# One matrix product per mamba group: three products of split parts in place of one in full fp32

## The chip, the cores and the metric

The kernel runs on one core of a Trainium2 chip. A core has a matrix engine (TensorE, PE in the profile), a vector engine (VectorE, DVE), a scalar engine (ScalarE, ACT), GpSimd (POOL) and a queue for transfers (SyncE, SP). Each takes its own instructions strictly in the order in which they stand in its queue; semaphores make one engine wait for another or for a transfer. The metric is device time in microseconds: 1594.79 us before (median of 3 runs, 1594.73 to 1595.04).

## The reference

A two-layer encoder on 256 tokens of width 2048: layer 1 is a mamba block, layer 2 a forgetting attention. The part that matters is the mamba block, in chunks of 64 tokens in the reference and of two tiles of 128 tokens in the kernel:

```python
proj = h @ w_in                       # z, x, B, C and dt
xbc = silu(conv(x, B, C))
...
cb = einsum('bclgn,bcsgn->bclsg', cm, bm)
y_diag = einsum('bclsgr,bcsgrp->bclgrp', cb[..., None] * lmat, xdt)
...
y_off = einsum('bclgn,bcgrpn->bclgrp', cm, prev) * exp(acs)[..., None]
...
y = gated_group_rmsnorm(y, z, norm_w)
return y @ w_out
```

There are 8 groups of 8 heads. All is fp32 and has to agree with the reference to fp32 accuracy.

## The kernel before

The work is a list of parts that `run` walks through. A part is a bundle of products on PE, of some 1.4 to 2.8 us, and weights are prepared three halves ahead: a transfer brings `raw` (or sums of weights, `sum_a`, `sum_b`, `sum_c`, which POOL's queue builds by adding transfers), ACT rounds it to the format fp32r into `wh`, DVE takes the rest, `wl = raw - wh`, and PE multiplies `wh` and `wl`. An fp32r product takes one pass on PE; three of them, high times high, high times low and low times high, stand for one product in fp32. `act_hi` and `dve_lo` are these two steps.

The side work of a mamba group, which lies between these products, is put off by `later(n, fn)`: it is issued n double steps of parts later. What stands in which order on an engine is then set by a scheduler, which walks through the program with its own estimate of times and puts an instruction where its inputs and its buffers are free; so a tile's buffer, too, sets an instruction's place. Buffers of a tag go round (`bufs`), and a writer waits until all who read the buffer's last tile are done.

A group g goes like this:

- B, C and four blocks of x are projected (`pst`), joined and convolved (`rest`, `cu`, `BT`, `CT`, `xT`); `rest` has 2 buffers.
- `load_acs(i)`, i = 0 to 3, lets POOL's queue load `acsB`: sums of decays of two heads, spread over the 128 partitions, 128x512 fp32, from a buffer in memory. The tag `acsB` has 2 buffers.
- `decay(i)`: ACT makes `ee` out of `acsB` with four activations (Relu, 128x128 each) and one Exp (128x512). The tag `ee` has 3 buffers. DVE multiplies it with `cb`.
- `y_pe(i)`: PE multiplies `ee` and `xd` in fp32 (`py`).
- `off_pe`: the product this document is about. For the second tile of 128 tokens, the part of the output that comes from the first tile: `pof = cb[:, 128:256].T @ xg`, 128x128 by 128x512, in fp32. `xg` is x times step and decay; the middle part of `cb` is C of the second tile times B of the first.
- `off_dve`: `pof` times a decay (`yo`) is added to `xa`.
- z is projected (`psa`), ACT takes its tanh (`zth`, two instructions), DVE makes `zs` of it; `gate(t)` adds `py` to `xa`, multiplies by `zs`, and ACT sums its squares (`junkg`, one for each tile of tokens); `norm` makes the factor `gv` on DVE and POOL; ACT scales `xa` twice; `out_pe` transposes `xa` on PE (`pyt`).

Parts of the next group's projections, and from the third group on of the output projection (`sum_units`, tiles `psx`, `psz`, `psv`), run on PE around all this. The mamba layer takes about the first 650 us.

Of the kernel before, what the change touches and what calls it, by code (L numbers as in the profile page):

```python
# [12 lines left out]
F32R = mybir.dt.float32r  # L13
# [4 lines left out]
P = 128  # L18
# [49 lines left out]
def hybrid_kernel(ctx: ExitStack, tc: tile.TileContext, a):  # L68
    nc = tc.nc

    def pool(name, bufs, **kw):
        return ctx.enter_context(tc.tile_pool(name=name, bufs=bufs, **kw))
# [6 lines left out]
    sp = pool("side", 2)  # L79
# [5 lines left out]
    lp = phase.enter_context(tc.tile_pool(name="mamba", bufs=1))  # L85
# [13 lines left out]
    def bank(p, name):  # L99
        return p.tile([P, 512], F32, tag=p.name, name=name)  # L100

    def act_hi(out, in_, scale=None):
        if scale is None:
            nc.scalar.activation(out, in_, AF.Copy)  # L104
        else:
            nc.scalar.activation(out, in_, AF.Copy, scale=scale)

    def dve_lo(out, in_, hi, scale=None):
        if scale is None:
            return nc.vector.tensor_tensor(out, in_, hi.bitcast(F32), op=ALU.subtract)  # L110
        return nc.vector.scalar_tensor_tensor(
            out, in_, scale, hi.bitcast(F32), op0=ALU.mult, op1=ALU.subtract)
# [10 lines left out]
    def later(n, fn):  # L123

        events.setdefault(now[0] + 2 * n, []).append(fn)
# [114 lines left out]
    def unit_both(src, n, x, post):  # L240


        u = {"src": src, "w": [None], "both": (2 * n, n)}

        def mm(h):
            if h == 0:
                u["ps"] = bank(psm, "pst")
            for k in range(8 * h, 8 * h + 8):
                product(u["ps"][:2 * n], u["w"][0][0][:, 2 * n * k:2 * n * k + 2 * n],
                        ktile(x(), k).rearrange("p i s -> p (i s)"), start=k == 0,  # L250
                        stop=k == KT - 1)

        parts = [{"u": u, "h": [0], "mm": lambda h=h: mm(h)} for h in range(2)]
        parts[1]["post"] = lambda: post(u["ps"])
        return parts
# [129 lines left out]
    def per_token(ps, n, scale, bias, done):  # L385


        vt = sp.tile([P, S], F32, tag="cu", name="vt")
        joined(vt[:2 * n, :], ps, scale)

        def rest():
            pt = bank(psa, "pvt")
            for t in range(T2):
                nc.tensor.matmul(pt[:, t * n:(t + 1) * n], vt[:2 * n, t * P:t * P + P],
                                 cst[:2 * n, C_S[n]:C_S[n] + n], start=True, stop=True)
            v = small.tile([P, T2, 64], F32, tag="v", name="v", bufs=1)[:, :, :n]
            nc.vector.tensor_tensor(
                v, pt[:, :T2 * n].rearrange("p (t h) -> p t h", t=T2),
                bias.unsqueeze(1).to_broadcast([P, T2, n]), op=ALU.add)
            done(v)  # L400
        later(2, rest)
# [151 lines left out]
    def group_units(g):  # L553
        st = {"acs": {}}
# [31 lines left out]
        def post_x(i):  # L586
            def post(ps):
                conv_silu(ps, 6 * g + 2 + i, f"xT{g}_{i}", lambda o: x_done(i, o))
                later(2 + wait, lambda: load_acs(i))
            return post  # L590
# [7 lines left out]
        def x_done(i, o):  # L598
            st[f"x{i}"] = o
            if g == 0:  # L600
                later(1 + wait, lambda: xa_pe(i))
                later(2 + wait, lambda: xa_dve(i))
            elif i % 2:
                st["first"], st["then"] = ((cb_pe,), (cb_dve, lambda: st["mul0"]())) if i == 1 else (
                    (lambda: y_pe(0), lambda: y_pe(1)), ())
                later(2, lambda: [f() for f in (lambda: xa_pe(i - 1), lambda: xa_pe(i),
                                                *st["first"])])
                later(3, lambda: [f() for f in (*st["then"], lambda: xa_dve(i - 1),
                                                lambda: xa_dve(i))])
            later(2 + wait + more, lambda: decay(i))  # L610
            if g == 0:
                later(4 + wait + more, lambda: y_pe(i))
            if i == 3:
                if g > 0:
                    later(5, lambda: [y_pe(2), y_pe(3)])
                late = wait + more or 1
                later(4 + late, off_pe)
                later(5 + late, off_dve)

        def xa_pe(i):  # L620
            st[f"pxa{i}"] = pt = bank(psa, "pxa")
            for t in range(T2):
                nc.tensor.transpose(pt[:, t * P:t * P + P], st[f"x{i}"][:, t * P:t * P + P],
                                    ident)

        def xa_dve(i):
            if i == 0:
                xa = lp.tile([P, 4 * (S + 1)], F32, tag="xa", name=f"xa{g}", bufs=2)
                st["xa"] = xa[:, :T2 * 512].rearrange("p (t c) -> p t c", t=T2)
                xd = lp.tile([P, 4 * (S + 1)], F32, tag="xd", name=f"xd{g}")  # L630
                st["xd"] = xd[:, :T2 * 512].rearrange("p (t c) -> p t c", t=T2)
                st["xg"] = lp.tile([P, 512], F32, tag="xg", name=f"xg{g}")
            c = slice(i * P, i * P + P)
            pt = st[f"pxa{i}"]
            pt4 = pt[:, :S].rearrange("p (t h d) -> p t h d", t=T2, h=2)
            d = dts[:, :, H0 + 2 * i:H0 + 2 * i + 2].unsqueeze(3).to_broadcast([P, T2, 2, HD])
            nc.vector.tensor_tensor(
                st["xd"][:, :, c].rearrange("p t (h d) -> p t h d", h=2), pt4, d, op=ALU.mult)
            nc.vector.tensor_tensor(
                st["xg"][:, c].rearrange("p (h d) -> p h d", h=2), pt4[:, 0],  # L640
                heads_of(gdt, i, 1), op=ALU.mult)
            nc.vector.tensor_tensor(
                st["xa"][:, :, c].rearrange("p t (h d) -> p t h d", h=2), pt4,
                heads_of(row[:, R_D:R_D + MH], i, T2), op=ALU.mult)

        def decay(i):
            ee = lp.tile([P, 2, T2, P], F32, tag="ee", name="ee", bufs=3)
            for j in range(2):
                h = H0 + 2 * i + j
                for t in range(T2):  # L650
                    nc.scalar.activation(ee[:, j, t, :], st["acs"][i][:, j, t * P:t * P + P],
                                         AF.Relu, scale=-1.0, bias=beta[:, t, h:h + 1])
            nc.scalar.activation(ee, ee, AF.Exp, scale=-1.0)

            def mul():
                cb = st["cb"].rearrange("p (b l) -> p b l", b=3)
                nc.vector.tensor_tensor(
                    ee, ee, cb[:, 0:3:2, :].unsqueeze(1).to_broadcast([P, 2, T2, P]), op=ALU.mult)
                st[f"m{i}"] = ee
            if g > 0 and i == 0:  # L660
                st["mul0"] = mul
            else:
                later(1, mul)

        def y_pe(i):
            if i == 0:
                st["py"] = [bank(psa, f"py{t}") for t in range(T2)]
            m = st[f"m{i}"]
            for j in range(2):
                hl = 2 * i + j  # L670
                c = slice(hl * HD, hl * HD + HD)
                for t in range(T2):
                    nc.tensor.matmul(st["py"][t][:, c], m[:, j, t, :], st["xd"][:, t, c],  # L673
                                     start=True, stop=True)

        def off_pe():
            st["pof"] = bank(psa, "pof")
            nc.tensor.matmul(st["pof"], st["cb"][:, P:2 * P], st["xg"], start=True, stop=True)  # L678

        def off_dve():  # L680
            yo = sp.tile([P, 512], F32, tag="zth", name="yo")
# [585 lines left out]


    groups = [group_units(g) for g in range(G)]
    parts = groups[0] + groups[1]  # L1270
    for g in range(0, SUMMED, 2):
# [5 lines left out]
    def out_f(g):  # L1277
# [3 lines left out]
    f = unit_both(a["wf_f"], FH, lambda: lay2["x"], lambda ps: later(1, lambda: per_token(  # L1281
        ps, FH, lay2["rstB"], row[:, R_F:R_F + FH], forget)))
# [98 lines left out]
```

## Time and profile before

| | us |
|---|---|
| runs, median (lowest to highest) | 1594.79 (1594.73 to 1595.04) |
| the profiled execution | 1594.61 |
| its span, first to last instruction | 1592.8 |
| PE busy | 1578.4 |
| DVE busy | 1333.6 |
| ACT busy | 1062.1 |
| POOL busy | 164.3 |

The profiled execution took 1.8 us more than its span and 0.18 us less than the median. The page gives busy times, the chain of work that ended last, and groups of instructions; views of the trace give the waits, the timeline of each engine, the chain piece by piece, and busy time by stretches. Times inside the trace are counted from the start of the span. A matrix product in fp32 shows as two instructions on PE, one in fp32r as one. L678 is line 678 of the kernel before.

### The profile page before, as it was taken

The numbers are of one execution on the slowest core, as the hardware profiler recorded it, in microseconds if no ns is written. First come the engines' busy times: TensorE is split into PE (matmuls) and PEld (weight loads), VectorE is DVE, ScalarE is ACT, GpSimd is POOL, SyncE is SP. The second block draws the span as 40 slices with busy tenths as digits, with TensorE's granted clock in tenths as the row PEclk, the third lists the DMA queues.
The fourth block names the chain that finished last, engine by engine and source line by source line (L and its number), as shares of the span: only waits on it lengthen the run. The fifth ranks groups of instructions, "written<-read, shape, count | busy, mean of one in ns | idle before, by whom it ended". The sixth has DMA issues, their size and how long they took to land.

```text
span 1592.8 us, 22603 instructions
## 1 busy us (share of the span) xinstructions
PE 1578.4 (99%) x7807; PEld 1328.2 (83%) x7807; DVE 1333.6 (84%) x2016; ACT 1062.1 (67%) x1624; POOL 164.3 (10%) x211
## 2 busy tenths in 40 slices
PE   8999999999999999999999999999999999999997
PEld 6888888888888888878888888888888888888886
DVE  6998989798979898798887887878878887888886
ACT  7677776767676765766776675666666666667663
POOL 0000111011100110011110110110110111011100
PEclk9999999999999999999999999999999999999999
DMA  9665798769986987579887887797886887888842
GB/s 360 214 215 185 185 275 220 260 177 275 221 265 174 274 220 237 188 168 260 262 236 254 220 214 250 224 247 215 221 258 189 249 256 180 237 263 239 266 156 80
DMA packets 100355, 361.76 MB, mean 227 GB/s; under 512 B 11504, under 2 KB 12144, under 8 KB 100112
## 3 DMA queue, kind: packets, MB, share of 16 engines
q1 hardware_dynamic: 75312, 270.82, 48.4%
q0 software_dynamic: 24784, 89.24, 29.3%
q8 instruction: 61, 1.00, 0.2%
q14 instruction: 54, 0.44, 0.1%
q10 hardware_dynamic: 144, 0.26, 0.1%
HBM read 358.08 MB, written 2.20 MB: 226 GB/s over the span
## 4 chain that ended last, share of the span: by engine, by line
PE 97%; DMA 2%; DVE 0%; issue 0%; ACT 0%; POOL 0%; SPq 0%; ACTq 0%; POOLq 0%
PE psa L130 24%; PE pst L130 16%; PE psx L130 12%; PE psz L130 10%; PE psv L130 9%; PE psu L130 8%; PE psy L130 8%; PE py L673 2%; PE pqk L1108 1%; PE psc L1126 1%; PE ppt L1162 1%; DMA cst<-in_consts 1%; DMA xs<-in_x 1%; PE pof L678 0%; PE po L1188 0%; PE psc L1124 0%
## 5 line engine op out<-in xcount | busy, mean ns | idle before, releaser
L104 ACT ACTIVATE wh<-raw 128x1024 fp32r<-128x1024 f32 (+1 forms) x371 | 391.8, 1058 | 209.9 <-PE psa L130 63.9
L110 DVE TENSOR_TENSOR wl<-raw,wh 128x1024 fp32r<-128x1024 f32 (+2 forms) x371 | 447.6, 1213 | 61.3 <-issue 30.0
L104 ACT ACTIVATE wh<-sum_a 128x1024 fp32r<-128x1024 f32 x176 | 185.8, 1057 | 134.1 <-PE psy L130 28.4
L110 DVE TENSOR_TENSOR wl<-sum_a,wh 128x1024 fp32r<-128x1024 f32 x176 | 214.9, 1223 | 61.8 <-PE psu L130 41.4
L130 PE MATMUL pst<-x,wh 128*128 128x512 f32 (+1 forms) x800 | 205.3, 397 | 3.0 <-ACT wh L104 1.8
L130 PEld LDWEIGHTS pst<-x,wh 128*128 128x128 f32 (+1 forms) x800 | 146.0, 189 | 33.7 <-ACT wh L104 2.5
L130 PE MATMUL psa<-wh,x 128*128 128x512 f32 x512 | 129.3, 392 | 0.0
L104 ACT ACTIVATE wh<-sum_b 128x1024 fp32r<-128x1024 f32 x88 | 93.3, 1060 | 51.9 <-PE psx L130 29.9
L110 DVE TENSOR_TENSOR wl<-sum_b,wh 128x1024 fp32r<-128x1024 f32 x88 | 106.6, 1221 | 10.4 <-issue 9.4
L130 PEld LDWEIGHTS pst<-x,wl 128*128 128x128 f32 x768 | 106.4, 191 | 9.8 <-DVE wl L110 1.6
L130 PEld LDWEIGHTS psa<-wh,x 128*128 128x128 f32 x512 | 95.4, 188 | 20.3 <-issue 0.5
L130 PE MATMUL pst<-x,wl 128*128 128x256 f32 x768 | 109.6, 284 | 0.4 <-DVE wl L110 0.4
L177 POOL DMA_DIRECT2D sum_a<-in_wf_s x64 | 56.0, 876 | 469.9 <-DVE wl L110 293.3
L130 PE MATMUL psz<-wh,x 128*128 128x512 f32 x256 | 100.4, 392 | 0.0
L130 PE MATMUL psv<-wh,x 128*128 128x512 f32 x256 | 99.8, 390 | 0.0
L130 PE MATMUL psu<-wh,x 128*128 128x512 f32 x256 | 99.7, 390 | 0.0
L130 PE MATMUL psy<-wh,x 128*128 128x512 f32 x256 | 99.7, 389 | 0.0
L766 DVE TENSOR_TENSOR xs<-psa,xs 128x512 f32<-128x512 f32 (+1 forms) x81 | 52.0, 680 | 31.7 <-PE psa L130 31.6
L130 PE MATMUL psa<-wh,ghf 128*128 128x512 f32 (+1 forms) x260 | 71.0, 392 | 0.0
L130 PE MATMUL psa<-wh,glf 128*128 128x512 f32 (+1 forms) x260 | 69.6, 386 | 0.0
L130 PE MATMUL psa<-wl,ghf 128*128 128x512 f32 (+1 forms) x260 | 69.6, 386 | 0.0
L130 PE MATMUL psa<-wl,x 128*128 128x512 f32 x256 | 69.0, 390 | 0.0
(360 smaller groups left out, 3251.8 us busy)
## 6 DMA issues: line engine op xcount, KB each, us to landing
raw<-in_wf_p SPq DMA_DIRECT2D x128, 512.0 KB, 4.8
raw<-in_wm_t SPq DMA_DIRECT2D x90, 512.0 KB, 4.9
raw<-in_wm_z SPq DMA_DIRECT2D x64, 512.0 KB, 5.7
sum_a<-in_wf_s POOLq DMA_DIRECT2D x64, 512.0 KB, 8.1
raw<-in_wf_o SPq DMA_DIRECT2D x64, 512.0 KB, 5.3
sum_a<-in_wm_s POOLq DMA_DIRECT2D x36, 512.0 KB, 6.4
sum_a<-in_wf_s SPq DMA_DIRECT2D x32, 512.0 KB, 7.3
sum_c<-in_wf_s SPq DMA_DIRECT2D x32, 512.0 KB, 5.7
```

What stands on the lines that cost most here:

```text
L104: nc.scalar.activation(out, in_, AF.Copy)
L110: return nc.vector.tensor_tensor(out, in_, hi.bitcast(F32), op=ALU.subtract)
L130: behind["PE"] = nc.tensor.matmul(*args, **kw).ins
L177: behind["POOL"] = nc.gpsimd.dma_start(u["sums"][name], src, accum_op=ALU.add).ins
L673: nc.tensor.matmul(st["py"][t][:, c], m[:, j, t, :], st["xd"][:, t, c], start=True, stop=True)
L766: nc.vector.tensor_tensor(c, pss[t][:, a:b], c, op=ALU.add)
L1108: nc.tensor.transpose(pt[:, n * P:n * P + P], st["qk"][:, t, c:c + FD], ident)
L1126: nc.tensor.matmul(ps[:, P:P + S], q[:, :P], k[:, P:], start=j == 0, stop=j == 2)
L1162: nc.tensor.transpose(pt[:, c:c + P], uu[:, c:c + P], ident)
```

## The change

`off_pe` multiplies split parts. A new step `off_split`, one double step ahead of it, makes them: ACT rounds `xg` into `xgh` and the middle part of `cb` into one half of `cbhl`, DVE takes the rests `xgl` and the other half. `xgh` and `xgl` are tiles of the tag `acsB`, whose two buffers they take after the group's four loads; `cbhl` is a tile of the tag `rest`. PE then does three fp32r products, which add up in `pof`.

```diff
+                later(3 + late, off_split)
                 later(4 + late, off_pe)
...
+        def off_split():
+            xs2 = [lp.tile([P, 512], F32R, tag="acsB", name=f"xg{i}", bufs=2) for i in "hl"]
+            c2 = sp.tile([P, 2, P], F32R, tag="rest", name="cbhl")
+            cb = st["cb"][:, P:2 * P]
+            act_hi(xs2[0], st["xg"])
+            act_hi(c2[:, 0], cb)
+            dve_lo(xs2[1], st["xg"], xs2[0])
+            dve_lo(c2[:, 1], cb, c2[:, 0])
+            st["off"] = (xs2, c2)
+
         def off_pe():
             st["pof"] = bank(psa, "pof")
-            nc.tensor.matmul(st["pof"], st["cb"][:, P:2 * P], st["xg"], start=True, stop=True)
+            xs2, c2 = st["off"]
+            for n, (i, j) in enumerate(((0, 0), (0, 1), (1, 0))):
+                nc.tensor.matmul(st["pof"], c2[:, i], xs2[j], start=n == 0, stop=n == 2)
```

The change adds rows on PE, ACT and DVE, and it moves others, since the loads of the next group's `acsB` find the two buffers taken until `off_pe` has read them. Three places, with buffer numbers in the names; line numbers are larger by 1 now, and by 13 behind the new step.

ACT in the second group (g = 1), from the tanh of z to the scaling of `xa`; the `ee` in it belong to the group after it. Before:

```order
L694 ACTIVATE zth_1508<-psa0_1269,hrst1_95 128x512
L694 ACTIVATE zth_1511<-psa1_1270,hrst1_95 128x512
L104 ACTIVATE wh_1579<-raw_1578 128x1024
L711 ACTIVATE junkg_1543,gsq_1514<-xa1_1286 128x512
L104 ACTIVATE wh_1613<-raw_1612 128x1024
L305 COPY rest_1568<-pst_1524 128x256
L711 ACTIVATE junkg_1576,gsq_1514<-xa1_1286 128x512
L535 ACTIVATE BT2_1572<-cu_1567,vec_85 128x256
L104 ACTIVATE wh_1643<-raw_1642 128x1024
L104 ACTIVATE wh_1680<-raw_1679 128x1024
L721 ACTIVATE xa1_1286<-xa1_1286,gv_1601 128x512 x2
```

The same place now, from the row behind the two `zth` to the second `junkg`:

```order
L652 ACTIVATE ee_1867<-acsB_1806,beta_99 128x128 x3
L104 ACTIVATE wh_1597<-raw_1596 128x1024
L652 ACTIVATE ee_1867<-acsB_1806,beta_99 128x128
L652 ACTIVATE ee_1938<-acsB_1865,beta_99 128x128
L654 ACTIVATE ee_1867<-ee_1867 128x512
L724 ACTIVATE junkg_1561,gsq_1532<-xa1_1295 128x512
L104 ACTIVATE wh_1631<-raw_1630 128x1024
L305 COPY rest_1586<-pst_1542 128x256
L652 ACTIVATE ee_1938<-acsB_1865,beta_99 128x128 x3
L652 ACTIVATE ee_2022<-acsB_1927,beta_99 128x128
L654 ACTIVATE ee_1938<-ee_1938 128x512
L535 ACTIVATE BT2_1590<-cu_1585,vec_85 128x256
```

The next row is the second `junkg`. Nine activations of the next group's first three `acsB` and two Exp stood ahead of the tanh before, and stand between it and the second `junkg` now.

POOL's queue at the end of the third group (g = 2), where the loads for the fourth group stand among the transfers that build summed weights. Before:

```order
L177 DMA sum_b_2057<-in_wm_s 128x1024
L594 DMA acsB_2691<-acs_d_102 128x512
L594 DMA acsB_2790<-acs_d_102 128x512
L177 DMA sum_b_2117<-in_wm_s 128x1024
L177 DMA sum_a_1758<-in_wm_s 128x1024
L594 DMA acsB_2888<-acs_d_102 128x512
L594 DMA acsB_3396<-acs_d_102 128x512
L177 DMA sum_a_1817<-in_wm_s 128x1024
```

Now:

```order
L177 DMA sum_b_2075<-in_wm_s 128x1024
L177 DMA sum_b_2135<-in_wm_s 128x1024
L177 DMA sum_a_1776<-in_wm_s 128x1024
L594 DMA acsB_2629<-acs_d_102 128x512
L594 DMA acsB_2718<-acs_d_102 128x512
L177 DMA sum_a_1835<-in_wm_s 128x1024
L594 DMA acsB_2817<-acs_d_102 128x512
L594 DMA acsB_2915<-acs_d_102 128x512
```

Before, the fourth group's first load stood further ahead and its second and third behind the first `sum_b`, and the last `acsB` in the rows is the fifth group's. Now the fourth group's first load stands behind the `sum_a` and waits for `off_pe`.

ACT at the same place, g = 2, before the first `zth`. Before:

```order
L104 ACTIVATE wh_2220<-sum_b_2057 128x1024
L104 ACTIVATE wh_2237<-raw_2236 128x1024
L104 ACTIVATE wh_2250<-sum_b_2117 128x1024
L104 ACTIVATE wh_2275<-raw_2274 128x1024
L104 ACTIVATE wh_2291<-sum_a_1758 128x1024
L694 ACTIVATE zth_2267<-psa0_1990,hrst1_95 128x512
```

Now, from behind the same `wh` of a `sum_b`:

```order
L652 ACTIVATE ee_2698<-acsB_2629,beta_99 128x128 x3
L104 ACTIVATE wh_2264<-raw_2263 128x1024
L652 ACTIVATE ee_2698<-acsB_2629,beta_99 128x128
L652 ACTIVATE ee_2798<-acsB_2718,beta_99 128x128
L654 ACTIVATE ee_2698<-ee_2698 128x512
L104 ACTIVATE wh_2277<-sum_b_2135 128x1024
L652 ACTIVATE ee_2798<-acsB_2718,beta_99 128x128 x2
L654 ACTIVATE ee_2798<-ee_2798 128x512
L104 ACTIVATE wh_2302<-raw_2301 128x1024
L652 ACTIVATE ee_2896<-acsB_2817,beta_99 128x128 x3
L104 ACTIVATE wh_2318<-sum_a_1776 128x1024
L707 ACTIVATE zth_2294<-psa0_2008,hrst1_95 128x512
```

The `ee` of three loads have moved in among the four `wh` ahead of the tanh. Groups 4 and 6 have the same order on ACT; in groups 3 and 5 the `ee` of three loads have moved in there as well.

## The prediction

> **What bounds the kernel now.** The page first: the busy times, the clock, the chain that ended last. Then one stretch of PE by itself.
>
> ```profile
> span 1592.8 us, 22603 instructions
> PE 1578.4 (99%) x7807; PEld 1328.2 (83%) x7807; DVE 1333.6 (84%) x2016; ACT 1062.1 (67%) x1624; POOL 164.3 (10%) x211
> PEclk9999999999999999999999999999999999999999
> 45.00:650.00 605.00, 605.00 (x3177) 1.00 0.78 225
> ```
>
> PE is busy in all 605 of the 605 us from 45 to 650, at the full granted clock. All eight of the products in question lie there. So PE's own work sets the time: work taken off PE shortens it, work put on the other engines costs nothing until something reaches PE late, and then it costs the whole wait. There is no wait of PE in this stretch that could be removed.
>
> **What PE gains.** The chain cut into pieces shows starts of work that really follow on each other, where the instructions' own durations overlap. The rows are start, us, what.
>
> ```profile
> 127.52 0.76 PE psa L130 x3
> ...
> 194.83 1.45 PE psz L130 x6
> ...
> 204.84 0.91 PE pof L678 x2
> 205.75 1.38 PE psz L130 x6
> 207.13 2.72 PE psa L130 x12
> ```
>
> One product in fp32 (two records) holds PE for 0.91 us. An fp32r product of the same size takes 2.72 / 12 = 0.227 us in a stream. The entry matters too: behind fp32 products (`py`, at 194.83) six fp32r products take 1.45, behind `pof` 1.38, in the stream 6 x 0.227 = 1.36. The new order is `py`, three products for `pof`, then six `psz`: 1.45 + 3 x 0.227 = 2.13, where 0.91 + 1.38 = 2.29 stood. That is 0.16 us a group, 1.3 us for eight. The row at 127.52 is the nearest to the new piece, three fp32r products with `py` on both sides: 0.76. By it the gain would be 0.15 a group; by the stream alone, 0.91 - 0.68 = 0.23, or 1.8 in all. I take 1.3. That three products are not cheaper than one is thereby out.
>
> **What ACT and DVE get on top.** The nearest rows to the four new instructions:
>
> ```profile
> L721 ACT ACTIVATE xa<-xa,gv x16: 706/708/725, 114.2 to 639.6; 128x512 f32<-128x512 f32 x16
> L651 ACT ACTIVATE ee<-acsB,beta x128: 381/387/404, 66.1 to 608.2; 128x128 f32<-128x128 f32 x128
> L682 DVE TENSOR_TENSOR yo<-pof,fdec x8: 685/692/692, 99.4 to 619.1; 128x512 f32<-128x512 f32 x8
> L639 DVE TENSOR_TENSOR xg<-pxa,gdt x32: 280/286/296, 69.5 to 608.8; 128x128 f32<-128x128 f32 x32
> 135.00:145.00 10.00, 4.25 (x6) 1.00 0.77 234
> 205.00:215.00 10.00, 7.54 (x9) 1.00 1.04 281
> 245.00:255.00 10.00, 10.00 (x16) 1.00 0.72 212
> ```
>
> ACT gets 0.71 + 0.39 = 1.1 us a group, DVE 0.69 + 0.29 = 1.0. The last three rows are DVE's busy time in ten us each. Beside `off_pe` (138 us in group 1, 205 in group 2) DVE has 2.5 to 5.7 us in ten to spare, so I cost the four at nothing. The third row says that the cover is gone 40 us later: a lateness that DVE carries to there stays.
>
> **What moves.** The split parts take both buffers of `acsB`, so the next group's four loads wait for `off_pe` in place of `ee`, and the scheduler has set the `ee` behind them: in group 1 among the gate's steps, in groups 2, 4 and 6 among four `wh` ahead of the tanh of z. No transfer on SP is moved. `cbhl` takes a buffer of `rest`, which the second copy after it wants back; PE has read it by then, so this costs nothing, and one copy's wait if not. On POOL the loads now stand behind a `sum_a`.
>
> ```profile
> POOL acsB L594: 120.1, 30
> DMA to landing us min/median/max: 3.5/5.4/9.7
> DMA to landing us min/median/max: 3.5/4.2/5.0
> ```
>
> The first row: POOL's queue already waited 120 us for ACT to free these buffers, and nothing came of it, since a load had a whole group's time. The second is a load's time from issue to landing over the run, the third between 130 and 143 us. The room is what is now lost. [...]
>
> **Group 1, worked out.** ACT, with PE's and POOL's rows at the end:
>
> ```profile
> 143.57 1.25 ACT L694 ACTIVATE zth<-psa,hrst 128x512 f32<-128x512 f32 x2
> 146.85 0.63 ACT L711 ACTIVATE junkg<-xa 128x512 f32<-128x512 f32 x1 [1.09 <-DVE xa L709]
> 147.48 1.05 ACT L104 ACTIVATE wh<-raw 128x1024 fp32r<-128x1024 f32 x1
> 148.43 0.35 ACT L305 COPY rest<-pst 128x256 f32<-128x256 f32 x1
> 150.06 0.63 ACT L711 ACTIVATE junkg<-xa 128x512 f32<-128x512 f32 x1 [1.28 <-DVE xa L709]
> 150.69 0.59 ACT L535 ACTIVATE BT<-cu,vec 128x256 f32<-128x256 f32 x1
> 128.79 1.28 ACT L651 ACTIVATE ee<-acsB,beta 128x128 f32<-128x128 f32 x4 [0.75 <-PE py L673]
> 206.57 0.62 ACT L653 ACTIVATE ee<-ee 128x512 f32<-128x512 f32 x1
> 154.03 1.34 ACT L721 ACTIVATE xa<-xa,gv 128x512 f32<-128x512 f32 x2 [0.57 <-DVE gv L718]
> 155.95 1.04 PE L728 MATMUL pyt<-cst,xa 128*128 128x128 f32 x8
> 152.13 1.61 POOL L117 TENSOR_TENSOR gv<-gv,nhalf 128x2 f32<-128x2 f32 x1 [9.23 <-DMA raw<-in_wm_t]
> ```
>
> Before, `xa` is scaled by 155.4 and PE wants it at 155.95: 0.6 us of room. Now, from the tanh's end at 144.8: three Relu (0.3 each), `wh` 1.0, two Relu, Exp 0.6, first `junkg` 0.65, `wh`, `rest` 0.35, three Relu: 150.7. Then a Relu of the third load. That load could be issued when the fourth Relu of the first was through, at 147.0, and lands 4.2 later: 151.2. Relu, Exp, `BT` 0.6, second `junkg` 0.7: 153.4, where 150.8 stood. DVE then makes `gv` with one `wl` of 1.2 us moved in between, and POOL's step takes 0.7 to 1.6: `xa` is scaled by 157.0 to 157.9. PE comes 0.3 earlier for the two products that it has saved by then. It waits 1.3 to 2.2; I take 1.8. Behind that the rest is late by nothing, as PE is late too.
>
> **Groups 2, 4 and 6.** Rows of ACT, PE and POOL's load:
>
> ```profile
> 209.58 1.04 ACT L104 ACTIVATE wh<-sum_b 128x1024 fp32r<-128x1024 f32 x1
> 221.22 0.63 ACT L711 ACTIVATE junkg<-xa 128x512 f32<-128x512 f32 x1 [0.92 <-DVE xa L709]
> 224.15 0.63 ACT L711 ACTIVATE junkg<-xa 128x512 f32<-128x512 f32 x1
> 227.15 1.34 ACT L721 ACTIVATE xa<-xa,gv 128x512 f32<-128x512 f32 x2 [0.45 <-DVE gv L718]
> 231.68 1.04 PE L728 MATMUL pyt<-cst,xa 128*128 128x128 f32 x8
> acsB<-acs_d POOLq DMA_DIRECT2D x1, 256.0 KB, 7.1
> DMA to landing us min/median/max: 8.1/8.1/8.1
> ```
>
> The last two rows are loads beside `off_pe` in group 2 and group 6: 7.1 and 8.1 us. The first load of group 3 can be issued at 205.6 and lands at about 212.7. ACT gets to its Relu at 210.6 and stands. From 212.7: three Relu, `wh`, two Relu, Exp, Relu, `wh`, two Relu, Exp, `wh`: 219.3. The third load, issued at 215.1 when the first is read, lands some 5 us later, at 220.1; three Relu, `wh`, two tanh: 223.3, where about 219.4 stood. `wh`, Relu, Exp, and the first `junkg` ends at 226.0 and not at 221.9, the second at 228.6 and not at 224.9. `xa` is scaled 3.7 us later, by 232.2, and PE wants it at 231.7 less 0.5: it waits about 0.6 if group 2's load lands as assumed; by a landing one us later, more by as much, and by one that takes 5.4, nothing. With the 8.1 of group 6 and a middle case for group 4, I take 0.6, 1.0 and 1.4, together 3.0. Groups 3 and 5 have the `ee` in the same place but no summed weights between; I cost them at nothing, with 1 us each as the upper end.
>
> **The sum.** -1.3 + 1.8 + 3.0 = +3.5 us, against the execution profiled: 1594.61 + 3.5 = 1598.1. The median of the runs lies 0.18 above that execution: 1598.3. The bounds: no wait at all, 1593.5, or 1593.0 with the larger gain; at the upper end 2.2 in group 1, 2.5 in each of the three, 1 each in 3 and 5, together 11.7 less 1.3: 1605.2.
>
> **Rivals.**
> - *The waits are covered.* ACT is busy 67% and could make good what it loses; the gate steps may start earlier than I place them. For it: 120 us of waits on POOL reached nobody. Against it: the room of 0.6 us in group 1. The time is 1593.5, not slower. It decides if `xa` is late by less than 0.6 there and by less than 3.2 (231.7 less 228.5) in group 2. Chance 0.2.
> - *Fast landings.* If each load landed before ACT gets to its Relu (within 5.0 us in group 2, 205.6 to 210.6, and within 3.7 in group 1, 147.0 to 150.7), ACT would stand nowhere. Then the second `junkg` of group 1 ends at 152.9, PE waits 0.8 to 1.7, say 1.3, and the tanh of group 2 ends at 220.4, one us late, which its room of 3.2 covers: -1.3 + 1.3, 1594.8 by the runs' median. [...] The landings of 3.5 to 9.7 us, and of 7.1 and 8.1 at the place, speak against it. Chance 0.08.
> - *DVE passes it on.* ACT's lateness of 4 us at 223 delays `wl` as well; DVE is full from 245 (10.00 of 10) and cannot catch up, so `wl` and `xT` reach PE late further on. Then each of groups 2, 4 and 6 costs some 3 us: -1.3 + 1.8 + 9 gives 1604.3. Against it: PE's wait at `pyt` takes most of that lateness off. Chance 0.12.
>
> **How the numbers follow.** The sum's own case has 0.6, from 1595.5 to 1601.5. What a measurement of this kernel tells from no change is about 0.2%, 3.2 us: 1591.6 to 1598.0. Of the 0.6 some 0.38 lies above it, with the 0.12 of DVE 0.5 for slower. The rest and the first two rivals are 0.46 for the same. A gain of over 3.2 us has no source in PE's pieces, at most 1.8; 0.04 for what I don't see. Range 1593.0 to 1604.5, which leaves out the far part of DVE's case and of the unseen.
>
> **What would show it.** PE's busy time down by about 1.3 us between 45 and 650. In the list of waits PE, or its weight loads, waiting for ACT's `xa` at `pyt`, in group 1 first (near 156 us), then near 232, 394 and 557. ACT's idle time before `ee`, ended by the load of `acsB`, up from before. `zth` of group 2 at 222 and not at 218. The prediction is wrong if `pyt` in group 1 starts at 155.7, or if PE's waits stand at `wl` or `xT`.

## The result, and the profile after

The changed kernel takes 1609.05 us (median of 5 runs, 1608.29 to 1611.19), the kernel before 1594.79 beside it (5 runs, 1594.18 to 1595.04). The ratio is 1.0094, with a 95% interval from 1.0084 to 1.0105: slower by some 14 us. The prediction was 1598.3, in a range up to 1604.5. The direction was right, the size was four times what I had worked out.

The profiled execution took 1608.78 us. Its span and busy times, and PE's stretch from 45 to 650 us (columns of the last row: the stretch, its length, busy time of PE, PEld, DVE, ACT and POOL with the instructions in brackets, PE's granted clock, DMA share, GB/s):

```profile
span 1607.0 us, 22653 instructions
PE 1582.0 (98%) x7815; PEld 1330.7 (83%) x7815; DVE 1338.8 (83%) x2032; ACT 1063.1 (66%) x1640; POOL 163.9 (10%) x211
45.00:650.00 605.00, 594.74 (x3116) 507.81 (x3116) 530.28 (x868) 408.51 (x655) 66.11 (x88) 0.99 0.77 221
```

PE, without a gap in these 605 us before, now has 10.3 us of gaps in them, and 61 fewer products got done (3116, 3177 before). The list of PE's waits over the whole span (us in total, times, longest) names them, besides small ones at the program's start and for weights:

```profile
PE psx L130 <- DVE xs L812: 7.4, 4, 3.3
...
PE py L674 <- ACT form L749: 1.2, 1, 1.2
PE psa L130 <- DVE cu L306: 0.9, 1, 0.9
PE pxa L624 <- DVE xT L545: 0.8, 1, 0.8
```

None of them is a wait for `xa` at `pyt`. PE waits at `psx`, a running sum of the output projection that DVE adds to `xs` several times while it grows: the next product into `psx` has to wait until DVE has read the sum so far. Group 2 shows the whole chain, in rows of POOL, ACT, DVE and PE (start, us, what, and in brackets the idle time before and what ended it):

```profile
206.41 1.13 POOL L594 DMA_DIRECT2D acsB<-acs_d  x2 [1.06 <-PE pof L691]
acsB<-acs_d POOLq DMA_DIRECT2D x2, 256.0 KB, 8.6
215.05 0.99 ACT L652 ACTIVATE ee<-acsB,beta 128x128 f32<-128x128 f32 x3 [4.39 <-DMA acsB<-acs_d]
223.38 1.24 ACT L707 ACTIVATE zth<-psa,hrst 128x512 f32<-128x512 f32 x2
224.08 1.29 DVE L708 SCALAR_TENSOR_TENSOR zs<-zth,psa 128x512 f32<-128x512 f32 x2 [1.29 <-ACT zth L707]
228.75 0.68 DVE L812 TENSOR_TENSOR xs<-xs,psx 128x512 f32<-128x512 f32 x1
229.58 0.70 PE L130 MATMUL psx<-wh,ghm 128*128 128x512 f32 x2 [2.07 <-DVE xs L812]
```

The loads are issued once `pof` is done and land 8.6 us later; ACT stands 4.4 us for them; the tanh starts at 223.4 and not at 218.1; DVE waits for it, and reads `psx` at 228.75, where it had at 223.97. The chain of work that ended last takes the same way here, and one piece of it is the load itself, 8.62 us from 206.41. The same places in the kernel before:

```profile
218.11 1.25 ACT L694 ACTIVATE zth<-psa,hrst 128x512 f32<-128x512 f32 x2
223.97 0.68 DVE L799 TENSOR_TENSOR xs<-xs,psx 128x512 f32<-128x512 f32 x1
226.13 0.63 PE L130 MATMUL psx<-wh,ghm 128*128 128x512 f32 x2
```

DVE was through at 224.65 and PE came at 226.13: a room of 1.5 us, less than the 3.2 at `pyt`.

How much later each engine stands is measured by the same instruction in both traces, its start now less its start before. For PE (`pxa` are its four transposes of x in a group):

| where | shift of PE before it, us | behind it | cost |
|---|---|---|---|
| group 1, third `pxa` to `pof` | -0.76 | +0.65 | 1.4 |
| group 2, `pof` to `pyt` | +0.72 | +5.14 | 4.4 |
| group 3, third `pxa` to `pyt` | +4.93 | +4.80 | -0.1 |
| group 4, `pof` to `pyt` | +4.80 | +6.52 | 1.7 |
| group 5, first to third `pxa` | +6.52 | +7.68 | 1.2 |
| group 6, up to `pof` | +7.56 | +9.07 | 1.5 |
| group 6, `pof` to `pyt` | +9.07 | +14.14 | 5.1 |

Behind group 6 the shift stays, +14.0 at the end of the mamba layer.

The 1.4 us of group 1 come the same way, from loads that wait for `off_pe` of group 0 (98 us). Rows of ACT, DVE, ACT and PE:

```profile
103.18 1.58 ACT L652 ACTIVATE ee<-acsB,beta 128x128 f32<-128x128 f32 x5 [1.03 <-DMA acsB<-acs_d]
106.75 0.48 DVE L540 SCALAR_TENSOR_TENSOR xT<-cu,vec,xT 128x255 f32<-128x255 f32 x1 [1.26 <-ACT xT L535]
127.95 0.98 ACT L749 ACTIVATE form<-pyt,vec 128x256 f32<-128x256 f32 x2 [0.21 <-DVE glm L110]
128.99 1.10 PE L674 MATMUL py<-xd,ee 128*128 128x64 f32 x8 [1.23 <-ACT form L749]
```

ACT stands for a load and has `ee` ahead of `xT`; DVE stands 1.26 us for `xT`, is then 1.7 us behind PE, and is busy for 14.3 of the 15 us from 113 to 128; `form`, which ACT makes of `pyt` for the output projection, comes behind it, and PE waits for `form`.

### The profile page after: what moved, and what is told of

The parts are those of the page before. It is cut to its first block, busy times and chain, and to the rows that moved or that the text cites. A ratio compares the mean times of both kernels' runs of the same rounds, so it can differ in the third digit from the quotient of the medians.

```text
span 1607.0 us, 22653 instructions
## 1 busy us (share of the span) xinstructions
PE 1582.0 (98%) x7815; PEld 1330.7 (83%) x7815; DVE 1338.8 (83%) x2032; ACT 1063.1 (66%) x1640; POOL 163.9 (10%) x211
## 4 chain that ended last, share of the span: by engine, by line
PE 86%; DVE 5%; DMA 5%; issue 2%; ACT 1%; POOL 0%; SPq 0%; ACTq 0%; POOLq 0%; DVEq 0%
PE psa L130 22%; PE psx L130 11%; PE pst L130 11%; PE psz L130 9%; PE psv L130 9%; PE psy L130 8%; PE psu L130 8%; DVE wl L110 2%; DMA acsB<-acs_d 2%; PE py L674 2%; PE pqk L1121 1%; PE psc L1139 1%; PE ppt L1175 1%; DMA sum_a<-in_wf_s 1%; DMA cst<-in_consts 1%
```

## The experiments

**Are the shared buffers the cost?** Three kernels. The first keeps all of the change, but `xgh` and `xgl` take buffers of the tag `zth`:

```diff
-            xs2 = [lp.tile([P, 512], F32R, tag="acsB", name=f"xg{i}", bufs=2) for i in "hl"]
+            xs2 = [sp.tile([P, 512], F32R, tag="zth", name=f"xg{i}") for i in "hl"]
```

> The three products and all four split instructions stay; the split parts of xg lie in buffers of the tag zth, so that acsB's two buffers go to loads alone, as in the kernel before. If the shared buffers of acsB are the cost (theory), everything but the gain on PE comes back: 1594.8 - 1.3 = 1593.5 us, at most 1596, no wait of PE at psx or pyt near 230, 395 and 564 us. If the split's own work on ACT and DVE (2.1 us a group) or the three products are the cost (rival), the time stays near 1609 and the same waits stand at the same places.

Measured: 1593.56 us (11 runs, 1592.51 to 1595.97), the kernel before 1595.14 beside it; ratio 0.999 (0.9982 to 0.9999). The loss is gone. What is left is PE's gain. PE's timeline in group 2, and its stretch from 45 to 650 us, in this kernel, and behind them two rows of PE's timeline in the kernel before:

```profile
202.98 1.90 PE L674 MATMUL py<-xd,ee 128*128 128x64 f32 x16
204.69 0.48 PE L691 MATMUL pof<-xgh,cbhl 128*128 128x512 f32 x1
...
206.82 1.98 PE L130 MATMUL psa<-wh,x 128*128 128x512 f32 x8
45.00:650.00 605.00, 604.63 (x3188) 518.64 (x3187) 541.95 (x884) 421.64 (x669) 67.44 (x89) 1.00 0.78 225
```
```profile
204.67 1.08 PE L678 MATMUL pof<-xg,cb 128*128 128x512 f32 x2
...
206.97 1.98 PE L130 MATMUL psa<-wh,x 128*128 128x512 f32 x8
```

From the start of `pof` to the next `psa` it is 206.82 - 204.69 = 2.13 us, where 206.97 - 204.67 = 2.30 stood: 0.17 a group, and 0.16 was predicted. At the end of the mamba layer PE's shift is -1.3 us. The split's own 2.1 us a group on ACT and DVE cost nothing. This version is the fastest of all that were run, though by no more than its interval can just tell from no change.

The second takes `zth` in groups 2, 4 and 6 alone:

```diff
+            p, tag, n = (sp, "zth", None) if g in (2, 4, 6) else (lp, "acsB", 2)
+            xs2 = [p.tile([P, 512], F32R, tag=tag, name=f"xg{i}", bufs=n) for i in "hl"]
```

> The split parts lie in buffers of the tag zth in groups 2, 4 and 6 alone; in the others they still take those of acsB. Landmarks on PE put 4.4, 1.7 and 5.1 us of the loss at these three groups, 11.2 together. The theory expects 1609.0 - 11.2 = 1597.8 us, with what is left from groups 1, 5 and the start of 6 (1.3, 0.9 and 0.9). If the places of the waits are only where a loss of other groups comes out, it is less than half of that: above 1603.

Measured: 1597.10 us (11 runs, 1593.19 to 1600.24), ratio 1.0014 (1.0005 to 1.0023). Three groups carry 12 of the 14 us; the table of shifts has 11.2 at these places, and the 1.2 at `cu` behind group 4 belongs to it.

The third holds `acsB`'s buffers in the same way, with plain copies of `xg` in them, and does the product in full fp32 (its edit in part):

```diff
-            for n, (i, j) in enumerate(((0, 0), (0, 1), (1, 0))):
-                nc.tensor.matmul(st["pof"], c2[:, i], xs2[j], start=n == 0, stop=n == 2)
+            for j in range(2):
+                c = slice(j * 256, j * 256 + 256)
+                nc.tensor.matmul(st["pof"][:, c], st["cb"][:, P:2 * P], xs2[j][:, c],
+                                 start=True, stop=True)
```

> The product is done in full fp32 as before, in two halves of 256 columns, from copies of xg that lie in the two tiles of acsB; so the buffers are held as in the changed kernel, with nearly the same work on ACT and DVE, but without the three fp32r products. If the held buffers are the cost: 1609 plus the 1.3 us of PE, 1608 to 1612. If the three products or their format are: near 1595.

Measured: 1616.2 us (4 runs, 1614.04 to 1620.18), ratio 1.0133 (1.0119 to 1.0147). So the products' form isn't the cost. It came out above what I expected: ACT stood longer than in the changed kernel (in group 2 6.75 us against 4.39), and PE waited six times at `psx`, 11.3 us in all. Why ACT stood longer here is open.

**`cbhl` in a buffer of its own.** `sp.tile(..., tag="rest", ...)` became `lp.tile(..., tag="cbhl", ...)`.

> cbhl has a buffer of its own instead of one of the tag rest; acsB is shared as in the changed kernel. If acsB is the cost: unchanged, 1608 to 1610 us. If the copies that wait for a buffer of rest are a part of it (rival), the wait of PE for xT and cu in groups 5 and 6 (0.8 and 0.9 us) goes, or more: 1607 and less.

Measured: 1609.98 us (4 runs, 1608.62 to 1610.45), ratio 1.009 (1.0076 to 1.0103). Unchanged; the buffer of `rest` costs nothing that can be measured. The rival's sign is there in part, since the waits at `xT` and `cu` in groups 5 and 6 are missing in this execution; but groups 1 and 4 lost more in it, and PE's shift at the end is again +14.1.

**ACT's order, with late loads.** The loads wait for `off_pe` as in the changed kernel, but the `ee` of the first three are held back. `make` issues the five activations of an `ee`, and `behind["ACT"]` is the last scaling of `xa`:

```diff
+            def make():
...
+            if g > 1 and i < 3:
+                with tc.issue_after(behind["ACT"]):
+                    make()
+            else:
+                make()
```

> The split parts still take acsB's buffers and the loads still wait for off_pe, but ACT's ee for the next group's first three loads are put behind the scaling of xa, out of the way of the tanh. Theory (ACT stands in order for a late load, and that is all the loss in groups 2, 4 and 6): 1609.05 - 11.2 = 1597.8, or 1595 if the small waits of groups 1, 5 and 6 go too. Rival: the late loads cost by themselves, since y_pe of the next group then gets ee late, and PE waits at py: above 1603.

Measured: 1593.94 us (11 runs, 1592.95 to 1595.03), ratio 0.9992 (0.9983 to 1.0001). The late loads cost nothing by themselves; ACT's standing for them does, since the tanh of z is queued behind. The `wh` of a `raw` that stands behind the load's first three Relu in the changed kernel starts at 215.9 us there, and at 211.5 with the `ee` held back. It came out 1 to 4 us below what I expected: the waits of groups 5 and 6 at `cu` and `xT` went as well, so these too had been the same lateness (the `ee` of groups 2 to 7 are held back). The wait at `py` in group 1, where none is held back, is still there, at 0.8 us. ACT in group 2 now:

```profile
218.76 1.25 ACT L713 ACTIVATE zth<-psa,hrst 128x512 f32<-128x512 f32 x2
227.80 1.34 ACT L740 ACTIVATE xa<-xa,gv 128x512 f32<-128x512 f32 x2 [0.45 <-DVE gv L737]
230.00 0.97 ACT L653 ACTIVATE ee<-acsB,beta 128x128 f32<-128x128 f32 x3
```

**The landing, and the moment of the release.** `nc.gpsimd.dma_start` of the loads became `nc.sync.dma_start`:

> The loads of acsB are issued by SP's queue instead of POOL's, where they stand behind summing transfers; buffers and PE's order are as in the changed kernel. Theory: the landing (8.6, 7.4 and 7.6 us in groups 2, 4 and 6) is what ACT stands for, and behind POOL's summing transfers it is long; on SP's queue some 4 to 5 us, so ACT is about 3 us less late and most of the 11.2 us goes: 1597 to 1601. Rival: the landing is as long there, or SP's queue, stopped by the load that waits for off_pe, brings raw late: 1606 or more, with waits of PE for wh.

Measured: 1611.99 us (4 runs, 1609.83 to 1613.08), ratio 1.0102 (1.0088 to 1.0116). My expectation fell. The first two loads land in 6.7 us in place of 8.6, and SP's queue stands while the third load waits for its buffer, with weights behind it (a row of the transfers, one of SP's timeline and one of ACT's):

```profile
acsB<-acs_d SPq DMA_DIRECT2D x2, 256.0 KB, 6.7
208.35 7.88 SPq L594 DMA_DIRECT2D acsB<-acs_d  x2
213.64 0.99 ACT L652 ACTIVATE ee<-acsB,beta 128x128 f32<-128x128 f32 x3 [3.98 <-DMA acsB<-acs_d]
```

ACT stands 4.0 us in place of 4.4, and then 0.7 more for the third load. The long landing wasn't due to the summing transfers on POOL's queue alone. What a shorter landing is worth this run doesn't tell, since the scheduler has changed ACT's order as well: in group 2 one `wh`, one Relu and one Exp more lie between the load and the tanh, which starts 17.9 us behind `pof`, as in the changed kernel (18.0). The rival's waits of PE for `wh` didn't come either; PE waits at `psx`, 2.6, 3.6 and 3.5 us.

In the next, `later(4 + late, off_pe)` became `later(5 + late, off_pe)`, and `off_dve` one more too:

> The changed kernel with off_pe (and off_dve) one double step later, 1.8 to 2.7 us of PE's work, so that the two acsB buffers come free that much later. Theory: ACT stands that much longer in groups 2, 4 and 6, DVE falls behind by as much more, and PE pays it in full: 1609.05 + 3 x (1.8 to 2.7) = 1614.5 to 1617; groups 3 and 5 may begin to pay too, some us more. Rival: only the place of the ee in ACT's order counts, not the moment of the release: 1608 to 1610.

Measured: 1611.08 us (5 runs, 1609.82 to 1616.15), ratio 1.0109 (1.0094 to 1.0124), between the theory and the rival. The profiled execution is the slowest of the five. In it `pof` starts 1.4 us later against its neighbours, not 1.8 to 2.7, but the tanh starts 0.3 us earlier in group 2 and only 0.6 and 0.7 later in groups 4 and 6, since the first loads land in 6.3, 6.7 and 6.8 us, where they took 8.6, 7.4 and 7.6. So the moment of the release counts for half at the most at the tanh. From the third `pxa` to `pyt` the three groups cost 4.1, 3.9 and 6.8 us, 14.7 together where it was 11.1; a part of these 3.6 us is PE's clock (below), whose mean over the span is 0.995 here and 0.997 in the changed kernel. The wait of group 1 at `py` is gone in this order; 1.8 us are lost between the first and third `pxa` of group 2 instead.

**Where PE pays.** The three additions at which PE waited are left out (the `post` of that term in groups 2, 4 and 6):

```diff
-                    if g == groups[-1]:
+                    if g == groups[-1] and (form, cp2) != (6, 0):
                         part["post"] = lambda name=name, reads=reads, add=add: [
```

> The changed kernel with three additions of DVE left out, one in each of groups 2, 4 and 6: the xs<-xs,psx behind which PE waited there. These terms of the sum are then added up by PE alone (the output lacks the interim sums' second use); PE's order is unchanged. Theory: PE waits for DVE's reading of psx, with 1.5 us of room, and not for xa at pyt. So the 11.2 us of the three groups (4.4, 1.7, 5.1) go, and a wait at pyt of 0.3 to 0.9 us stands in each of them instead, which is what the prediction had worked out: 1609.05 - 11.2 + 1.8 = 1599.6, from 1598 to 1601 us. Rival: ACT's lateness reaches PE in any case, by wl, zs or xa; then 1605 or more.

Measured: 1603.57 us (5 runs, 1602.44 to 1605.10), ratio 1.0053 (1.0040 to 1.0066). It lies between the theory's range and the rival's. Only half of the 11 us goes, and not to `pyt`: PE's shift from `pof` to `pyt` grows by 1.2, -0.1 and 0.0 us in the three groups. Behind groups 2 and 4 most of what isn't paid there is paid some 45 us later, at `cu` (a row of the list of PE's waits, and one of PE's timeline):

```profile
PE psa L130 <- DVE cu L306: 3.0, 2, 1.5
276.01 1.19 PE L130 MATMUL psa<-wh,x 128*128 128x512 f32 x4 [1.51 <-DVE cu L306]
```

One instruction of DVE, 33 us behind the tanh, tells why. Its rows in DVE's timeline, one fence each for the kernel before, the changed one, and this one:

```profile
251.54 0.43 DVE L306 TENSOR_TENSOR cu<-pst,rest 128x256 f32<-128x256 f32 x1
```
```profile
256.37 0.43 DVE L306 TENSOR_TENSOR cu<-pst,rest 128x256 f32<-128x256 f32 x1
```
```profile
257.17 0.41 DVE L306 TENSOR_TENSOR cu<-pst,rest 128x256 f32<-128x256 f32 x1
```

DVE is 4.8 us late in the changed kernel, as at 228 us, and 5.6 in this one. It is full here (10.00 of 10 us from 245 on, the prediction's third row of windows; 15.00 of 15 from 245 to 260 in both other kernels), so a lateness that it has taken on stays to a tenth of a microsecond until about 260 us. PE meets it in the changed kernel at `psx`, in this one at `cu`.

Behind group 6 it doesn't. Counted from one `pof` to the next, groups 2, 4 and 6 cost 4.2, 2.9 and 5.0 us in the changed kernel and 3.4, 1.9 and 0.2 in this one: most of the gain is group 6's. DVE was 3.2 us behind PE there too, and was level with it some 30 us later at next to no cost to PE. The difference is DVE's spare time. Its busy time in 30 us behind each of the three places, in the kernel before:

```profile
230.00:260.00 30.00, 29.08 (x48) 1.00 0.82 210
393.00:423.00 30.00, 29.33 (x48) 1.00 0.86 216
555.00:585.00 30.00, 26.90 (x41) 1.00 0.85 222
```

It has 0.9 and 0.7 us to spare behind groups 2 and 4, and 3.1 behind group 6.

**DVE lighter.** To see whether DVE could make it good if it had time, two of three taps of the convolution are left out in groups 3 and 5, once without the three additions and once with them:

```diff
-            for j in (1, 2, 3):
+            for j in (1, 2, 3) if ct // 6 not in (3, 5) else (1,):
```

> As the run without the three additions, and DVE also leaves out two of the three taps of the convolution in groups 3 and 5 (12 instructions of 0.4 us, 4.7 us in each, between 8 and 45 us behind the place). Theory: DVE, some 3 us behind PE from 220 us on and full from 245 on, can't make it good, and PE pays later, at cu, pcb and pxa (2.2 us after group 2, 2.1 after group 4 in the trace of that run). With the taps left out DVE makes it good: 1603.6 - 4.3 = 1599.3 us, from 1598 to 1600.5. Rival: the late waits have another cause (weights, transfers): 1602 or more.

Measured: 1604.16 us (6 runs, 1600.24 to 1605.88), ratio 1.0053 (1.0039 to 1.0066): no gain, and my expectation missed. In its profiled execution DVE is 2.9 us behind PE at 230 us and level with it by 260, and from group 2's `pyt` to group 3's third `pxa` PE loses 0.5 us where it had lost 2.2: that is as the theory has it. But after group 4 it loses 1.7, against 2.1, and in this execution group 1 alone lost 4.7, with 2.1 of it the very wait that the prediction had put there (PE's timeline):

```profile
159.67 2.37 PE L741 MATMUL pyt<-cst,xa 128*128 128x128 f32 x8 [2.07 <-ACT xa L734]
```

So group 2 bears the theory out. Group 4 doesn't follow because of a transfer, which was the rival. DVE was level with PE by 430 us, and then stood for ACT, which stood for weights (a row of ACT's timeline and one of DVE's):

```profile
432.88 1.06 ACT L104 ACTIVATE wh<-raw 128x1024 fp32r<-128x1024 f32 x1 [3.17 <-DMA raw<-in_wm_z]
434.46 0.48 DVE L540 SCALAR_TENSOR_TENSOR xT<-cu,vec,xT 128x255 f32<-128x255 f32 x1 [1.45 <-ACT xT L535]
```

That `raw` landed 8.8 us after its issue, in the kernel before 7.0, in the changed one 7.5.

> The changed kernel with the same 24 taps left out on DVE. Theory: PE pays at psx, 5 to 10 us behind the tanh and ahead of the taps, so nothing is saved there; only what PE pays later goes (1.15 us after group 4, at pcb and cu): 1609.05 - 1.2 = 1607.9 us, from 1606.5 to 1608.5. Rival: DVE's load as a whole makes the waits; with 9.4 us less of it they shrink at psx as well: 1604 or less.

Measured: 1608.13 us (5 runs, 1606.69 to 1609.75), ratio 1.0081 (1.0068 to 1.0093), as expected. PE waits four times at `psx`, as in the changed kernel, and no more at `cu` (the list of its waits):

```profile
PE psx L130 <- DVE xs L812: 7.4, 4, 2.6
```

**The clock.** In the changed kernel PE's shift grows by 4.4 us in group 2, though its waits there are 0.4 and 2.1. The rest lies behind the second wait. Windows of the changed kernel around the waits of group 2 and group 4:

```profile
228.00:231.00 3.00, 1.42 (x6) 1.18 (x7) 2.81 (x6) 2.85 (x6) 0.07 (x1) 0.93 0.84 261
231.00:234.00 3.00, 3.00 (x9) 2.33 (x8) 2.32 (x4) 2.07 (x3) 0.64 (x1) 0.50 0.71 253
397.00:400.00 3.00, 3.00 (x18) 2.65 (x17) 2.59 (x4) 2.29 (x3) 0.38 (x1) 1.00 0.72 228
```

Behind group 2's wait the granted clock is 0.50 for 3 us and PE does 9 products in place of 18; behind group 4's, of 1.6 us, it is 1.00. To take the clock's loss away, seven products by zeros were put ahead of each of the three waits (the edit in part):

```diff
+            for _ in range(7 if u.get("fill") == h else 0):
+                product(ps, nought, ktile(v, 0).rearrange("p i s -> p (i s)"), start=False, stop=False)
```

> The changed kernel with seven more products on PE, by a matrix of zeros, ahead of each of the three long waits at psx (groups 2, 4 and 6): 7 x 0.227 = 1.6 us of work at a time at which PE waits anyhow (2.3, 1.7 and 3.4 us). In the trace products behind the waits of groups 2 and 6 take 0.43 us instead of 0.23, nine or ten of them, at a granted clock of 0.50: 1.9 us each, and none behind that of group 4. Theory: the wait itself takes the clock down, so with the wait cut by 1.6 us no clock is lost: 1609.05 - 3.8 = 1605.2, within 1 us. Rival: the low clock has another cause and the products are hidden in the wait: 1609; or they delay PE: 1611 to 1614.

Measured: 1609.92 us (5 runs, 1606.68 to 1611.88), ratio 1.0089 (1.0076 to 1.0101). That is the rival's time, not the theory's 1605.2. But the three waits are 0.7 to 1.0 us now, and no product behind them is slow (PE's timeline in group 2):

```profile
229.67 1.75 PE L132 MATMUL pst<-x,nought 128*128 128x512 f32 x7
...
233.22 0.70 PE L132 MATMUL psx<-wh,ghm 128*128 128x512 f32 x2 [0.85 <-DVE xs L816]
```

PE loses 2.8, 3.0 and 3.1 us at the three places, 8.8 in all where it was 11.2. But DVE is still 1.9 us behind PE after each, and PE pays for that later (another 1.0 us after group 2 and 2.1 after group 4, at `cu`; after group 6 nothing). From one `pof` to the next the three groups cost 3.8, 5.1 and 3.0 us, where it was 4.2, 2.9 and 5.0. So in group 2 the low clock took time that was mostly lost already, as it let DVE come level; behind group 6, where DVE has time to spare, the 2.0 us come back. Group 4 had no low clock to lose, and cost 2.2 more, with ACT standing 4.3 us for its load instead of 3.2. Group 1 lost 3.5 in this execution instead of 1.4, 1.4 of it by seven slow products behind a wait of 1.7. Behind the shorter waits, of 0.7 to 1.0 us, the clock thus stayed up in this run; what that is worth it doesn't show.

## Why the prediction was wrong, point by point

- **PE's gain, -1.3 us.** Right: 0.17 a group where 0.16 was taken, a shift of -1.3 us in the trace with the buffers apart, and 1593.56 us measured, 1.6 below the kernel before beside it.
- **The split's work on ACT and DVE, and `cbhl`, at nothing.** Right, by the same run and by the one with a buffer for `cbhl`.
- **The chain up to the tanh in groups 2, 4 and 6.** Right in kind, and near in size for group 2: the load was taken to land in 7.1 us and landed in 8.6, ACT was to reach the tanh at about 222 and did at 223.4. The experiment on ACT's order shows that this is all of the cause from group 2 on.
- **What PE pays for it, 3.0 us.** This is the step that failed. It measured 4.4 + 1.7 + 5.1 = 11.2. I took the lateness, 3.7 us, less a room of 3.2 at `pyt`, as if ACT's `xa` were the only thing that PE wants from this chain. But ACT's lateness is DVE's too, and DVE reads `psx` for PE, with a room of 1.5. DVE was 4.2, 3.1 and 4.8 us behind PE in groups 2, 4 and 6, and PE waited 2.4, 1.6 and 3.3 us at `psx`: DVE's lateness less the room, to 0.3 us. That is 7.4 of the 11.2. The other 3.8 lie almost all behind the waits of groups 2 and 6, where PE's clock was low (0.50), a term that the prediction didn't have. And a room only puts the payment off where DVE has no spare time: in group 4 PE paid another 1.2 at `cu`. A slip in the sum is small beside this: 232.2 less 231.2 is 1.0 for group 2, not 0.6.
- **Group 1, 1.8 us.** 1.4 was lost there, near in size by luck: PE waited 1.2 us at `py` for ACT's `form`, and nothing at `pyt`. The source is the loads behind group 0's `off_pe`, at which the prediction didn't look. The wait at `pyt` did turn up in other executions (2.1 us in one). With no shared buffers there is none at `py` either.
- **Groups 3 and 5 at nothing.** Right at the place. The 2.7 us (1.2 and 1.5 in the table) that PE lost between group 5's first `pxa` and group 6's `pof` come with the waits at `cu` and `xT`, and go when ACT doesn't stand.
- **The rivals.** "DVE passes it on" was the mechanism, at 0.12 and 1604.3 us, though it looked for the waits at `wl` and `xT`, and most of them were at `psx`. It was put against PE's wait at `pyt`, which I thought takes the lateness off; and it had 3 us a group, which is what DVE's lateness comes to in the mildest of the three. "The waits are covered" fell with the 11.2 us, and so did "Fast landings": 8.6, 7.4 and 7.6 us at the three places.
- **What would show it.** ACT's idle time before `ee` and the late `zth` are in the trace as foretold. PE's waits at `pyt` are not, and PE's busy time over the span went up by 3.6 us (1582.0, 1578.4 before): work at a low clock counts as busy too (3.00 of 3 us from 231 to 234, at 0.50), so busy time alone doesn't show the gain.

## What to carry to other kernels

When a tile borrows another tag's buffers, the cost here was not the copy (2.1 us a group on ACT and DVE, and 1593.56 us with the buffers apart); it was every later writer of that tag, and whatever was queued in order behind the load for which the engine stood (4.4 us on ACT in group 2). If that lateness reaches an engine which is full for the next stretch, don't subtract a room at one consumer and stop there. Follow the late engine until it has spare time of its own: what it can't make good until then arrives at the bounding engine, as behind groups 2 and 4, and taking away one wait moves most of it to the next; what it can make good costs nothing, as behind group 6 without the additions (0.2 us). List all that the bounding engine wants from the late engines, interim reads of its own sums among them, and let the one with the least room set the place.

## What the hardware showed that I had not expected

Behind two of PE's waits in the changed kernel, 2.07 us in group 2 and 3.34 in group 6, the granted clock fell to 0.50. A 128x512 product in fp32r took 0.43 us there in place of 0.23. PE's rows ahead of group 6's wait and behind it, and its windows at both places (columns: the stretch, its length, PE's busy time, granted clock, DMA share, GB/s):

```profile
557.61 1.98 PE L130 MATMUL pst<-x,wh 128*128 128x512 f32 x8
563.87 0.70 PE L130 MATMUL psx<-wh,ghm 128*128 128x512 f32 x2 [3.34 <-DVE xs L812]
565.49 3.41 PE L130 MATMUL pst<-x,wh 128*128 128x512 f32 x8
230.60:234.00 3.40, 3.40 (x10) 0.50 0.71 253
565.12:568.50 3.38, 3.38 (x10) 0.50 0.70 246
```

The clock stood at 0.50 from 230.6 to 234.0 us and from 565.1 to 568.5, 3.41 us each time, and fell 1.0 and 1.2 us behind the end of the wait. At half the rate 3.41 us are an estimated 1.7 us of PE's work lost. Behind the changed kernel's waits of 1.59 us at `psx` (group 4) and 1.23 at `py` (group 1) it stayed at 1.00.

PE's timelines of other runs, by the products behind a wait (slow are those that take up to twice as long):

| run | waits of PE with slow products behind them, us | without |
|---|---|---|
| plain copies in `acsB`'s buffers | 2.36, 2.55 | 0.99, 1.17, 1.97, 2.28 |
| `cbhl` in a buffer of its own | 1.96, 1.99 | 1.88 |
| without the additions, DVE lighter | 2.07 | |
| products by zeros, group 2 | | 0.85 |

With `cbhl` in a buffer of its own the first two products behind group 4's wait of 1.96 us already took 0.93 in place of 0.70. So the length of a wait doesn't settle it alone: 1.96 us had slow products behind them and 2.28 had none. What else settles it was not shown.
